# Two output products as seven block products with sums built in DRAM, and state-space tiles four slots apart

## The chip, the cores and the metric

One core of a Trainium2 chip runs one layer of a decoder trunk in float32. The metric is device microseconds of one execution; the median of three runs stands for a kernel. TensorE multiplies, VectorE and ScalarE (ACT) do elementwise work, GpSimd (POOL) does a little, SyncE (SP) issues the DMA transfers. The engines work through their instructions in order, each on its own, and wait for each other by semaphores.

## The reference, cut to what matters

Sequence T = 512, model width D = 1024, hidden width 2816.

```python
z = rms_norm(x, norm_mix) @ w_in                # u | conv | q k v | three gates
merged = (g[..., 0:D] * (y_ssm @ w_branch[0]) + g[..., D:2*D] * (y_conv @ w_branch[1])
          + g[..., 2*D:] * (y_attn @ w_branch[2]))
x = x + merged @ w_out
hf = rms_norm(x, norm_ffn) @ w_ffn_in
x = x + (silu(hf[..., :FFN]) * hf[..., FFN:]) @ w_ffn_out
x = x + sigmoid(rms_norm(x, norm_ple) @ w_ple_gate) * (p @ w_ple_proj)
return rms_norm(x, norm_final)
```

`y_ssm` is a complex-diagonal state-space model over time with a gated output, `y_conv` a short convolution, `y_attn` a sliding-window attention.

## The kernel before, in words

**Products.** Every float32 operand of TensorE is split in a high part (`hi`, a cast to float32r on ACT) and a low part (`lo`, the subtraction on VectorE), and a product is three matmuls: high x high, high x low, low x high (`mm3`, L247; `td_mm`, L1213).

**Weight stream.** `add_slab` lists slabs of at most 1 MB in the order of use; `emit_load` (L179) issues their DMA on SP into one of two `raw` buffers; `emit_split` (L187) casts one half (128 x 1024) on ACT (L206) and sets its subtraction on VectorE (L207) four pumps later. A pump is one k step of a tile, three matmuls. Four buffers hold split halves during the first part; from w_out on, three more. A half is split as soon as a buffer is free: `take`, `group`, `ahead` and `retire` count it. So SP runs ahead of the work by two raw buffers and the split halves.

**Order of the work.** It is written out by hand. `later(d, fn)` puts a piece of work d pumps later into an engine's queue, `peq` holds small TensorE pieces that a pump puts between the matmuls of a stage, and `slot()` marks the steps of the branch stages: one slot after each gate tile or branch pair, 27 before the GLU, each eight pumps.

**State-space tiles.** Four tiles of 128 channels (`ssm_gen`, L957) run beside the branch stages, begun at slots 0, 5, 10 and 15 (L1127) and taken one step further by every slot. A step each: loads of `tb` and `uu`; the table E; the table W with the load of `cs` and the transposes; the matmuls into `vps` with the rotation and the scan behind them (`vsw`, `G`, `R`, `gsw`, `sv`); two steps later the copy of `Dg` on ACT (L1075); then the output matmuls `y_one` (L1082, L1084), after which SP stores `sy` (L1092), loads `un` and, waiting for the stores, loads `yr` (L1098); four steps after that `yc` and its GELU. After the slots the gated output (GLU) of the state-space branch, the last gates and its branch product follow.

**w_out and w_ffn_out.** `td_gemm` (L1230) computes [token, d] products: for each half n of the 1024 columns, four token tiles of 128, kn steps of k, three matmuls of 512 columns a step. For n = 0 the four tiles share each weight half, for n = 1 a tile is finished before the next one (where a norm follows) so that the tile's RMS norm (`Norm.pre`, L1253) begins at once: square on ACT (L1261), mean on VectorE (L1264), power -0.5 on POOL (L1265), scale on VectorE (L1272), transposes on TensorE (L325), high and low parts. `accum` (L1209) adds a finished tile into `xr` (L1211). w_out has kn = 8; the SwiGLU has hidden tiles in chunks of 8, 8 and 6, each chunk a run of w_ffn_in tiles (`g` halves, silu, product) and a `td_gemm` with w_ffn_out. `xr` is loaded from x when the buffers of the branch stage are free (L1205).

Of the kernel before, what the change touches and what calls it, by code (L numbers as in the profile page):

```python
# [25 lines left out]
WARM = 3  # L26
PREP_RATE = 1.7
# [48 lines left out]
def hybrid_trunk_kernel(  # L76
# [44 lines left out]
    def add_slab(ap, k, n, axis):  # L121
        s = len(slabs)
        slabs.append(dict(ap=ap, k=k, n=n, raw=None))
        cnt = 2 if k * n == 2048 else 1
        for i in range(cnt):
            halves.append(dict(s=s, i=i, cnt=cnt, axis=axis, hl=None))
# [31 lines left out]
    for n in range(2):  # L158
        for kk in range(2):
            add_slab(kn(w_out[0][kk * 512:kk * 512 + 512, n * 512:n * 512 + 512]), 4, 512, "k")  # L160
    CHUNKS = [(0, 8), (8, 8), (16, 6)]
    for h0, hn in CHUNKS:
        for j in range(h0, h0 + hn, 2):
            for ab in range(2):
                c0 = ab * FFN + j * 128
                add_slab(kn(w_ffn_in[0][:, c0:c0 + 256]), 8, 256, "n")
        for n in range(2):
            for k0 in range(0, hn, 4):
                kq = min(4, hn - k0)
                r0 = (h0 + k0) * 128  # L170
                add_slab(kn(w_ffn_out[0][r0:r0 + kq * 128, n * 512:n * 512 + 512]), kq, 512, "k")
# [5 lines left out]
    state = dict(pump=0, delay=False, split=0, load=0, next=0, top=3, slot=0, pools=[hla] * 4)  # L177

    def emit_load():  # L179
        s = slabs[state["load"]]  # L180
        state["load"] += 1
        t = rawp.tile([128, 2048], F32, tag="raw", name="raw")
        v = t[:, 0:s["k"] * s["n"]].rearrange("p (k n) -> p k n", k=s["k"])
        sp.dma_start(out=v, in_=s["ap"])
        s["raw"] = v

    def emit_split():  # L187
# [5 lines left out]
        k, n, i = s["k"], s["n"], h["i"]  # L193
        if h["cnt"] == 1:
            src = s["raw"]
        elif h["axis"] == "n":
            n //= 2
            src = s["raw"][:, :, i * n:(i + 1) * n]
        else:
            k //= 2  # L200
            src = s["raw"][:, i * k:(i + 1) * k, :]
        pl = state["pools"][state["slot"] % len(state["pools"])]
        state["slot"] += 1
        hi = pl.tile([128, 1024], F32R, tag="hi", name="hi").rearrange("p (k n) -> p k n", k=k)
        lo = pl.tile([128, 1024], F32R, tag="lo", name="lo").rearrange("p (k n) -> p k n", k=k)
# [60 lines left out]
    def pump(tick=True):  # L266
        if tick:
            state["pump"] += 1
            run_due(state["pump"])
# [117 lines left out]
    def prep_gen(tp):  # L387
        # per-channel vectors: ssm_d (4 tiles) and the conv taps (3 x 4 tiles)
# [59 lines left out]
    def prep_fine(tp, lt, ldt, T1, T2, tabs):  # L448
# [73 lines left out]
        # coefficients  # L522
# [85 lines left out]
    # the tensor engine's clock rises only under load  # L608
# [347 lines left out]
    # chunks of 4 tokens; channels of a group pair and the time in the chunk share the partitions  # L956
    def ssm_gen(ct):  # L957
# [69 lines left out]
        # the two row halves of the array write to banks of their own  # L1027
# [52 lines left out]
        def y_one(a):  # L1080
# [16 lines left out]
            yr = sp_.tile(SC, F32, tag="yb", name="yr", bufs=1)  # L1097
            sp.dma_start(out=yr, in_=sy_d[rows, :].rearrange("p (i c) -> p i c", i=4))  # L1098
            svs["un"], svs["yr"] = un, yr
# [3 lines left out]
        yield  # L1103
        yield
        yield
        yield
        un, yr = svs["un"], svs["yr"]
# [19 lines left out]
    SSM_SLOTS = {0: 0, 5: 1, 10: 2, 15: 3}  # L1127
# [17 lines left out]
    def branch(d0, sgs, yh, yl, mode, mh=None, ml=None):  # L1145
        hl = take()
        for i in range(2):
# [8 lines left out]
            if mode == 2:  # L1156
                split_ap(merged[:, d], mh[:, d], ml[:, d])
# [11 lines left out]
    drain()  # L1169
    ysh, ysl = ybox[0]  # L1170
# [16 lines left out]
    mst = ExitStack()  # L1187
    mhp = open_pool(mst, "mhl", side="right")
    mh = mhp.tile([128, KD, T], F32R, tag="mh", name="mh")
    ml = mhp.tile([128, KD, T], F32R, tag="ml", name="ml")  # L1190
    sg1 = gates()
    branch(0, sg0, yfh, yfl, 2, mh, ml)
    branch(2, sg1, yfh, yfl, 2, mh, ml)
    for d0 in (4, 6):
        branch(d0, gates(), yfh, yfl, 2, mh, ml)
# [4 lines left out]
    xp = open_pool(ctx, "xres")  # L1200
    hlb = open_pool(ctx, "hlb", 3)
    state["pools"] = [hla] * 4 + [hlb] * 3
    state["slot"] = 4
# [14 lines left out]
    def td_outer_k(ah, al, kn_, n):  # L1218
        pss = [ps_z() for _ in range(4)]
        for h in range(kn_ // 2):  # L1220
            hi, lo = take()
            for t in range(4):
                for k in range(2):
                    kk = 2 * h + k
                    td_mm(pss[t], ah, al, kk, slice(t * 128, (t + 1) * 128), hi, lo, k, kk == kn_ - 1)
                    pump()
        for t in range(4):
            accum(t, n, pss[t])

    def td_gemm(ah, al, kn_, pre_fn=None):  # L1230
        td_outer_k(ah, al, kn_, 0)
# [190 lines left out]
```

## Time and profile before

| | us |
|---|---|
| runs | 894.74, 895.66, 896.30 (median 895.66) |
| span of the profiled execution, first to last instruction | 892.6 |
| the execution's own time beside its span | not given apart; the median is 3.06 above the span |
| TensorE busy | 874.4 (98% of the span) |
| VectorE, ACT, POOL busy | 491.1, 341.0, 95.9 |
| w_out stage | about 424 to 470 |
| SwiGLU stage | about 471 to 838 |

How to read it: a matmul's duration in the profile is pipelined, its interval to the next one is its price. Idle time stands in brackets behind an instruction with what ended it. A wait for several things is put down to the last. Where an instruction's engine has other work in its queue, the instruction waits its turn though all that it needs is there.

### The profile page before, as it was taken

Reading aid. Unit: us, or ns where it says so; the run is one execution under the profiler, and the core shown is the slowest. Engines: PE = TensorE matmul, PEld = TensorE weight load, DVE = VectorE, ACT = ScalarE, POOL = GpSimd, SP = SyncE. Lnnn points to the kernel's source line nnn. Section 1 sums busy time; section 2 is a strip of 40 time slices with the busy share of each in tenths; the row PEclk is TensorE's granted clock in tenths of the full one; section 3 lists DMA queues with packets and bytes.
Section 4 is the critical chain, followed back from the end, with each engine's and each line's share of the span. In section 5 each row is a group of like instructions: output and inputs, shape, how many; then the busy total and the mean of one; then the engine's idle time right before and its main releaser. Section 6 shows DMA issues by size and latency. Waiting matters only on the chain.

```text
span 892.6 us, 10527 instructions
## 1 busy us (share of the span) xinstructions
PE 874.4 (98%) x4143; PEld 715.2 (80%) x4143; DVE 491.1 (55%) x737; ACT 341.0 (38%) x546; POOL 95.9 (11%) x86
## 2 busy tenths in 40 slices
PE   8999999999999979999999999999999999999997
PEld 6988787877777758888889888888888888888886
DVE  3789698948588585554545433333333333334654
ACT  5665556445443343433334322212222212222533
POOL 1030061713123030000000000000000000000000
PEclk9999999999999989999999999999999999999998
DMA  8756511253634523223813322222225332233002
GB/s 300 216 189 218 195 59 30 66 173 113 178 95 156 156 94 107 95 79 134 284 46 107 130 94 95 95 95 94 95 95 211 99 100 87 72 120 110 29 1 94
DMA packets 84849, 107.25 MB, mean 120 GB/s; under 512 B 6120, under 2 KB 66176, under 8 KB 84288
## 3 DMA queue, kind: packets, MB, share of 16 engines
q1 hardware_dynamic: 84800, 106.59, 36.5%
q8 instruction: 32, 0.52, 0.2%
q14 instruction: 17, 0.14, 0.1%
HBM read 94.83 MB, written 11.55 MB: 119 GB/s over the span
## 4 chain that ended last, share of the span: by engine, by line
PE 77%; DVE 10%; issue 4%; ACT 3%; DMA 3%; SPq 1%; POOL 1%; POOLq 0%; DVEq 0%; ACTq 0%
PE z L248 17%; PE z L249 16%; PE z L250 16%; PE z L1216 8%; PE z L1215 8%; PE z L1214 8%; DVE lo L207 1%; DVE s_t L839 1%; DMA xt<-in_x_dram 1%; PE t L325 1%; DVE s_t L812 1%; DMA raw<-in_w_in_dram 1%; POOL gsw L1063 1%; ACT s_t L826 1%; PE t L1084 1%
## 5 line engine op out<-in xcount | busy, mean ns | idle before, releaser
L248 PE MATMUL z<-h,hi 128*128 128x512 f32 (+1 forms) x776 | 298.6, 385 | 0.0
L207 DVE TENSOR_TENSOR lo<-raw,hi 128x1024 fp32r<-128x1024 f32 x142 | 177.6, 1253 | 216.2 <-ACT hi L206 216.1
L249 PE MATMUL z<-l,hi 128*128 128x512 f32 (+1 forms) x776 | 292.2, 377 | 0.0
L250 PE MATMUL z<-h,lo 128*128 128x512 f32 (+1 forms) x776 | 292.1, 376 | 0.0
L206 ACT CAST hi<-raw 128x1024 fp32r<-128x1024 f32 x142 | 148.2, 1047 | 133.1 <-PE z L1216 87.2
L248 PEld LDWEIGHTS z<-h,hi 128*128 128x128 f32 x776 | 146.8, 189 | 29.9 <-issue 3.7
L250 PEld LDWEIGHTS z<-h,lo 128*128 128x128 f32 x776 | 146.7, 189 | 27.6
L249 PEld LDWEIGHTS z<-l,hi 128*128 128x128 f32 x776 | 147.0, 189 | 24.7
L1214 PE MATMUL z<-hi,gh 128*128 128x512 f32 x176 | 69.5, 395 | 0.0
L1216 PE MATMUL z<-hi,gl 128*128 128x512 f32 x176 | 69.1, 393 | 0.0
L1215 PE MATMUL z<-lo,gh 128*128 128x512 f32 x176 | 69.1, 392 | 0.0
L1265 POOL TENSOR_TENSOR rs<-ms,nhalf 128x1 f32<-128x1 f32 x8 | 4.4, 550 | 487.2 <-DVE ms L1264 487.2
L244 ACT CAST gh<-sil 128x512 fp32r<-128x512 f32 x22 | 13.6, 620 | 86.0 <-DVE sil L1319 86.0
L248 PE MATMUL z<-yh,hi 128*128 128x512 f32 x112 | 45.1, 403 | 0.0
L249 PE MATMUL z<-yl,hi 128*128 128x512 f32 x112 | 44.2, 395 | 0.1
L250 PE MATMUL z<-yh,lo 128*128 128x512 f32 x112 | 44.2, 395 | 0.0
L1310 ACT ACTIVATE sil<-z 128x512 f32<-128x512 f32 x22 | 13.2, 598 | 75.4 <-PE z L250 75.4
L1319 DVE TENSOR_TENSOR sil<-z,sil 128x512 f32<-128x512 f32 x22 | 15.2, 691 | 46.8 <-PE z L250 46.8
L1216 PEld LDWEIGHTS z<-hi,gl 128*128 128x128 f32 x176 | 33.1, 188 | 7.5
L1215 PEld LDWEIGHTS z<-lo,gh 128*128 128x128 f32 x176 | 33.1, 188 | 7.4
L1214 PEld LDWEIGHTS z<-hi,gh 128*128 128x128 f32 x176 | 33.1, 188 | 7.3
L1211 DVE TENSOR_TENSOR xr<-z,xr 128x512 f32<-128x512 f32 x32 | 21.5, 687 | 15.6 <-PE z L1216 15.5
(258 smaller groups left out, 1058.5 us busy)
## 6 DMA issues: line engine op xcount, KB each, us to landing
raw<-in_w_in_dram SPq DMA_DIRECT2D x23, 1024.0 KB, 5.5
raw<-in_w_ffn_in_dram SPq DMA_DIRECT2D x22, 1024.0 KB, 5.2
raw<-in_w_ffn_out_dram SPq DMA_DIRECT2D x10, 1024.0 KB, 5.0
raw<-in_w_branch_dram SPq DMA_DIRECT2D x12, 512.0 KB, 3.4
cs<-tb SPq DMA_DIRECT2D x4, 1024.0 KB, 5.2
raw<-in_w_out_dram SPq DMA_DIRECT2D x4, 1024.0 KB, 5.8
raw<-in_w_ple_gate_dram SPq DMA_DIRECT2D x4, 1024.0 KB, 5.1
xt<-in_x_dram SPq DMA_DIRECT2D x4, 512.0 KB, 9.4
```

What stands on the lines that cost most here:

```text
L206: act.copy(out=hi, in_=src)
L207: todo = [lambda: dve.tensor_tensor(lo, src, hi.bitcast(F32), ALU.subtract)]
L244: act.copy(out=hi, in_=src)
L248: pe.matmul(ps, wh, ah, start=first, stop=False)
L249: pe.matmul(ps, wh, al, start=False, stop=False)
L250: pe.matmul(ps, wl, ah, start=False, stop=last)
L1211: dve.tensor_tensor(dst, ps, dst, ALU.add)
L1214: pe.matmul(ps, ah[:, kk, ts], hi[:, k, ns], start=(kk == 0), stop=False)
L1215: pe.matmul(ps, ah[:, kk, ts], lo[:, k, ns], start=False, stop=False)
L1216: pe.matmul(ps, al[:, kk, ts], hi[:, k, ns], start=False, stop=last)
L1310: act.activation(out=s, in_=ps, func=AF.Silu)
L1319: dve.tensor_tensor(sil[i], ps, sil[i], ALU.mult)
```

## The change

Write a product A B with A cut in four blocks by token half and by even or odd 128-row tile of k, and B in four by the same k and by column half n. Seven products of blocks, with sums of blocks on either side, give all four blocks of the result (Winograd's form); the seven results go with signs into two to four accumulators in PSUM and from there into `xr`.

- Left side: `forms` splits, for each pair of 128-row tiles, seven blocks of 128 x 256 in place of two of 128 x 512, three of them the blocks themselves and four sums on VectorE. It stands where `split_ap` stood for `merged` and for the SwiGLU product.
- Right side: four sums of weight blocks, t1 to t4, are built in DRAM by transfers on POOL's queue, eight for each of the four products (w_out and three chunks): two copies, two adding transfers on them, a copy of t1 into t2, an adding one, a copy of t2 into t4, an adding one. After the state-space tiles are drained, one is issued every 12 pumps; before the first slab of a product is loaded, all eight of it are issued.
- `block_product` takes the place of `td_gemm`: seven products of two token tiles and kt = 4, 4, 4, 3 steps, each with a slab of its own (two halves; 2 and 1 steps for kt = 3). Where a norm follows, the norms of token tiles 0 and 1 are begun after the fifth product and those of 2 and 3 after the seventh, four pumps apart.
- Four buffers of split halves stay until w_ple_gate, where three more are opened. The gain of the last norm and `ppt` are loaded after the last block product, not within the second chunk.
- State-space tiles begin at slots 0, 4, 8 and 12; `yr` is loaded a step after `un`, and `yc` comes three steps after the output matmuls in place of four.

```diff
+SUM_EVERY = 12
+NORM_GAP = 4
...
+    A11, A12, A22, FD, S2, S3, S4 = range(7)
+    ORDER = (A11, FD, S2, S4, S3, A12, A22)
+    ORDER_NORM = (A11, FD, S2, S4, A12, S3, A22)
+    def add_block_product(w, r0, kt, order):
...
+        op(t1, blk(0, 1))
+        op(t3, blk(0, 1))
+        op(t1, blk(0, 0), True)
+        op(t3, blk(1, 1), True)
+        op(t2, t1)
+        op(t2, blk(1, 1), True)
+        op(t4, t2)
+        op(t4, blk(1, 0), True)
+        sums.append(ops)
+        right = {A11: blk(0, 0), A12: blk(1, 0), A22: t4, FD: t1, S2: t2, S3: t3, S4: blk(1, 1)}
+        for f in order:
+            add_slab(right[f], kt, 512, "k", 8 * len(sums))
...
     def emit_load():
+        while n_sum - len(sum_ops) < s["need"]:
+            sum_ops.popleft()()
...
     def pump(tick=True):
+            if state["sums"] and sum_ops and state["pump"] % SUM_EVERY == 0:
+                sum_ops.popleft()()
...
         for a in range(4):
             peq.append(lambda a=a: y_one(a))
         yield
+        yr = sp_.tile(SC, F32, tag="yb", name="yr", bufs=1)
+        sp.dma_start(out=yr, in_=sy_d[rows, :].rearrange("p (i c) -> p i c", i=4))
         yield
         yield
-        yield
...
-    SSM_SLOTS = {0: 0, 5: 1, 10: 2, 15: 3}
+    SSM_SLOTS = {0: 0, 4: 1, 8: 2, 12: 3}
...
+    def forms(g, i):
+        sums = fmp.tile([128, 4, 256], F32, tag="sums", name="sums")
+        g11, g12, g21, g22 = (g[:, h, o:o + 256] for o in (0, 256) for h in range(2))
+        split_ap(g[:, :, 0:256], fh[:, 0:2, i], fl[:, 0:2, i])
+        dve.tensor_tensor(sums[:, 0], g21, g22, ALU.subtract)
+        dve.tensor_tensor(sums[:, 1], sums[:, 0], g11, ALU.subtract)
+        dve.tensor_tensor(sums[:, 2], g11, g21, ALU.subtract)
+        dve.tensor_tensor(sums[:, 3], g12, sums[:, 1], ALU.add)
+        split_ap(sums, fh[:, 3:7, i], fl[:, 3:7, i])
+        split_ap(g22, fh[:, 2, i], fl[:, 2, i])
...
+    PRODUCTS = {A11: (0, True, ((1, 0, 0),)), FD: (1, True, ((1, 1, 1),)), S2: (0, False, ((-1, 0, 1),)),
+                S4: (1, False, ((1, 0, 1),)), S3: (0, False, ((-1, 1, 1),)), A12: (2, True, ((1, 0, 0),)),
+                A22: (0, False, ((1, 1, 0),))}
+    PRODUCTS_NORM = {**PRODUCTS, S3: (0, False, ((-1, 1, 1), (1, 1, 0))), A22: (3, True, ((1, 1, 0),))}
+    def block_product(kt, norm=None):
...
+                for t in range(2):
...
+                        pe.matmul(ps, fh[:, f, kk, ts], hi[:, k], start=st, stop=False, skip_group_check=True)
+                        pe.matmul(ps, fh[:, f, kk, ts], lo[:, k], start=False, stop=False, skip_group_check=True)
+                        pe.matmul(ps, fl[:, f, kk, ts], hi[:, k], start=False, stop=last, skip_group_check=True)
+                        pump()
+                    if last:
+                        for sign, th, n in goes:
+                            dst = xr[:, 2 * th + t, n * 512:(n + 1) * 512]
+                            dve.tensor_tensor(dst, ps if sign > 0 else dst, dst if sign > 0 else ps,
+                                              ALU.add if sign > 0 else ALU.subtract)
+                retire(h0)
+            if norm is not None and i in (4, 6):
+                for t in range(2):
+                    norm.pre(2 * (i // 5) + t, NORM_GAP * t)
...
-    td_gemm(mh, ml, 8, nf.pre)
+    block_product(4, nf)
...
-            td_gemm(gh, gl, hn, npl.pre)
+        block_product(hn // 2, npl if ci == 2 else None)
```

## Rows read from the trace of the kernel before

**Rows 1.** The page's table: busy us (share of the span), instructions of each engine.

```profile
PE 874.4 (98%) x4143; PEld 715.2 (80%) x4143; DVE 491.1 (55%) x737; ACT 341.0 (38%) x546; POOL 95.9 (11%) x86
```

**Rows 2.** L1214 in two stages (ns min/median/max, first, last start); timeline with transposes.

```profile
L1214 PE MATMUL z<-hi,mh x64: 388/393/477, 424.0 to 469.5; 128*128 128x512 f32 x64
...
L1214 PE MATMUL z<-hi,gh x64: 389/392/398, 560.8 to 604.3; 128*128 128x512 f32 x64
...
457.77 0.39 PE L1216 MATMUL z<-hi,ml 128*128 128x512 f32 x1
458.00 0.60 PE L325 MATMUL t<-cst,xn 128*128 128x128 f32 x4
458.36 0.47 PE L1214 MATMUL z<-hi,mh 128*128 128x512 f32 x1
```

**Rows 3.** Waits of TensorE: us in total, times, longest.

```profile
PE t L1082 <- ACT Dg L1075: 4.5, 1, 4.5
```

**Rows 4.** Timeline of TensorE: an undisturbed tile, and around that wait.

```profile
219.89 0.50 PE L248 MATMUL z<-h,hi 128*128 128x512 f32 x1
...
221.37 0.50 PE L248 MATMUL z<-h,hi 128*128 128x512 f32 x1
...
319.26 0.39 PE L248 MATMUL z<-h,hi 128*128 128x512 f32 x1
...
324.61 0.80 PE L1082 MATMUL t<-uu,Dg 128*128 128x128 f32 x2 [4.49 <-ACT Dg L1075]
...
333.72 0.39 PE L248 MATMUL z<-h,hi 128*128 128x512 f32 x1
```

**Rows 5.** Windows: PE, PEld, DVE, ACT, POOL busy us (x), PEclk, DMA share, GB/s.

```profile
290.00:300.00 10.00, 10.00 (x52) 8.08 (x52) 9.54 (x12) 5.64 (x11) 1.44 (x1) 1.00 0.12 25
...
320.00:330.00 10.00, 5.23 (x17) 3.32 (x17) 7.63 (x10) 5.27 (x9) 4.13 (x3) 0.68 0.33 105
```

**Rows 6.** Timeline of SP's issues and of ACT before the wait.

```profile
295.16 4.91 SPq L1092 DMA_DIRECT2D sy<-ys  x8
...
301.42 0.34 SPq L1098 DMA_DIRECT2D yr<-sy  x1
...
302.28 0.43 SPq L184 DMA_DIRECT2D raw<-in_w_in_dram  x1
...
310.03 1.05 ACT L206 CAST hi<-raw 128x1024 fp32r<-128x1024 f32 x1 [12.39 <-DMA raw<-in_w_in_dram]
```

**Rows 7.** Groups by form: out<-in, count | busy us, mean ns | idle before.

```profile
L207 DVE TENSOR_TENSOR lo<-raw,hi 128x1024 fp32r<-128x1024 f32 x142 | 177.6, 1253 | 216.2 <-ACT hi L206 216.1
L206 ACT CAST hi<-raw 128x1024 fp32r<-128x1024 f32 x142 | 148.2, 1047 | 133.1 <-PE z L1216 87.2 <-DMA raw<-in_w_in_dram 19.8 <-PE z L249 16.3
...
L1211 DVE TENSOR_TENSOR xr<-z,xr 128x512 f32<-128x512 f32 x32 | 21.5, 687 | 15.6 <-PE z L1216 15.5
...
L245 DVE TENSOR_TENSOR l<-t,h 128x512 fp32r<-128x512 f32 x24 | 15.9, 684 | 2.4 <-ACT h L244 2.4
...
L1272 DVE SCALAR_TENSOR_TENSOR xn<-xr,rs,g 128x1024 f32<-128x1024 f32 x8 | 10.3, 1285 | 3.8 <-POOL rs L1265 3.6
...
L1265 POOL TENSOR_TENSOR rs<-ms,nhalf 128x1 f32<-128x1 f32 x8 | 4.4, 550 | 487.2 <-DVE ms L1264 487.2
```

**Rows 8.** xr: issue (SP's timeline), landing (the page), VectorE's adds (line L1211).

```profile
424.14 0.37 SPq L1205 DMA_DIRECT2D xr<-in_x_dram  x1
...
xr<-in_x_dram SPq DMA_DIRECT2D x1, 2048.0 KB, 7.9
...
L1211 DVE TENSOR_TENSOR xr<-z,xr x32: 678/691/693, 443.2 to 840.3; 128x512 f32<-128x512 f32 x32
```

**Rows 9.** All slab loads (tile raw): us from issue to landing.

```profile
DMA to landing us min/median/max: 3.2/5.2/11.6
```

**Rows 10.** Windows with xr's load and of the first w_ffn_out chunk (columns as rows 5).

```profile
427.50:430.00 2.50, 2.50 (x12) 2.01 (x11) 1.88 (x2) 2.48 (x3) 0.00 (x0) 1.00 1.03 418
...
560.50:605.00 44.50, 44.50 (x195) 36.30 (x194) 15.66 (x17) 8.92 (x9) 0.00 (x0) 1.00 0.33 106
```

More of the change, by code (lines that the diff above doesn't have):

```diff
@@ L119, in hybrid_trunk_kernel, with add_slab @@
     slabs = []
-    def add_slab(ap, k, n, axis):
+    def add_slab(ap, k, n, axis, need=0):
         s = len(slabs)
[L123 to L126, printed above, removed]
+        slabs.append(dict(ap=ap, k=k, n=n, raw=None, need=need))
+        if k * n <= 1024:
+            parts = [(0, k, 0, n)]
+        elif axis == "n":
+            parts = [(0, k, i * (n // 2), n // 2) for i in range(2)]
+        else:
+            k1 = (k + 1) // 2
+            parts = [(0, k1, 0, n), (k1, k - k1, 0, n)]
+        for q in parts:
+            halves.append(dict(s=s, part=q, hl=None))
     def kn(ap):
@@ L166, in hybrid_trunk_kernel @@
                 add_slab(kn(w_ffn_in[0][:, c0:c0 + 256]), 8, 256, "n")
[L167 to L171, printed above, removed]
+        add_block_product(w_ffn_out[0], h0 * 128, hn // 2, ORDER_NORM if hn == 6 else ORDER)
     for n in range(2):
@@ L176, in hybrid_trunk_kernel @@
     due = {}
-    state = dict(pump=0, delay=False, split=0, load=0, next=0, top=3, slot=0, pools=[hla] * 4)
+    state = dict(pump=0, delay=False, split=0, load=0, next=0, top=3, slot=0, pools=[hla] * 4, sums=False)
+    sum_ops = deque()
+    for ops in sums:
+        sum_ops.extend(ops)
+    n_sum = len(sum_ops)
     def emit_load():
@@ L1169, in hybrid_trunk_kernel @@
     drain()
+    state["sums"] = True
     ysh, ysl = ybox[0]
@@ new lines, in hybrid_trunk_kernel @@
+    PRODUCTS_NORM = {**PRODUCTS, S3: (0, False, ((-1, 1, 1), (1, 1, 0))), A22: (3, True, ((1, 1, 0),))}
+    def block_product(kt, norm=None):
+        banks = {}
+        for i, f in enumerate(ORDER if norm is None else ORDER_NORM):
+            bk, first, goes = (PRODUCTS if norm is None else PRODUCTS_NORM)[f]
+            if first:
+                banks[bk] = [(ps_t if bk == 2 else ps_z)() for _ in range(2)]
+            for q in range(2):
+                h0 = group(1)
+                if q == 0:
+                    ahead()
+                hi, lo = halves[h0]["hl"]
+                k0, kc = halves[h0]["part"][0:2]
+                for t in range(2):
+                    ps, ts = banks[bk][t], slice(t * 128, (t + 1) * 128)
+                    for k in range(kc):
+                        kk = k0 + k
+                        st = first and kk == 0
+                        last = kk == kt - 1
+                        pe.matmul(ps, fh[:, f, kk, ts], hi[:, k], start=st, stop=False, skip_group_check=True)
[11 more added lines that the diff above has]
+                    norm.pre(2 * (i // 5) + t, NORM_GAP * t)
@@ L1318, in hybrid_trunk_kernel @@
                     ps = z_tile()
[L1319 to L1327 removed]
+                dve.tensor_tensor(g[:, i], ps, g[:, i], ALU.mult)
+            forms(g, j // 2)
+        block_product(hn // 2, npl if ci == 2 else None)
     fst.close()
+    fmst.close()
+    hlb = open_pool(ctx, "hlb", 3)
+    state["pools"] = [hla] * 4 + [hlb] * 3
+    state["slot"] = 4
     ep = open_pool(ctx, "ple")
+    gain = load_gain(norm_final, ep)
+    ppt = ep.tile([128, 4, D], F32, tag="ppt", name="ppt")
+    for t in range(4):
+        sp.dma_start(out=ppt[:, t], in_=pp_d[t * 128:(t + 1) * 128, :])
     xg = ep.tile([128, 4, D], F32, tag="xg", name="xg")
```

110 lines of the change are left out of this document (30 added, 80 removed).

## The prediction

> **What bounds the kernel now.** I read the busy table first: TensorE is busy 874.4 of the 892.6 us of the span, every other engine under 56% [rows 1]. Only two things can then gain: fewer matmuls, or an end to a stretch in which TensorE stands still. The second view is one matmul line over one stage. In w_out 192 matmuls run, and the 64 of the first kind start between 424.0 and 469.5 us; 189 intervals less four groups of norm transposes (four matmuls each; they stretch an interval from 0.23 to 0.59 us, so 0.36 a group) give (45.5 - 1.4) / 189 = 0.233 us each. In the first w_ffn_out chunk 43.5 / 189 = 0.230 us [rows 2]. The 0.39 us shown as duration of one is pipelined and is no price. The third view is TensorE's waits: one is large, 4.5 us before the output matmuls of a state-space tile (L1082), waiting for the ACT copy of Dg [rows 3]. The timeline shows what it cost: from 319.26 to 333.72 us TensorE did one triple and four pairs of tile unit and triple. Such a pair takes 221.37 - 219.89 = 1.48 us where nothing waits, so the work is worth 0.69 + 4 x 1.48 = 6.6 us and took 14.5: **7.9 us lost** [rows 4]. The slice around it has a granted clock of 0.68: after the idle 4.5 us part of it ran at 1.2 instead of 2.4 GHz, which is the other 3.4 us [rows 5].
>
> Why it waited: SP stood in order behind the stores of the tile before (sy, issued from 295.16), then waited for their landing before yr, then issued cs, a 1 MB load, and only at 302.28 the next weight slab. ACT, in order too, waited 12.39 us for that slab and copied vsw, gsw and Dg of the last tile late [rows 6].
>
> **The change, part by part.**
>
> *Matmuls.* Seven products of 2 token tiles x kt x 3 replace eight. w_out: 168 for 192. w_ffn_out: 7 x 2 x 11 x 3 = 462 for 528. 24 x 0.233 + 66 x 0.230 = 5.6 + 15.2 = **-20.8 us**, all of it on the path.
>
> *State-space tiles every four slots, yr one step later, yc one earlier.* Tile 3 now begins at slot 12, not 15. Its cs load is issued in the step in which the former tile's output matmuls are only queued, so ahead of the sy stores; the wait for sy comes a slot later, behind weight loads. This takes out both things that stood ahead of the late slab. Bounds: 0 (the wait moves to another tile) to 7.9 us. I take **-7.9**, since the row names one chain and both its causes move. Speaking against: VectorE is 95% busy in a slice of this stage [rows 5], and the same work now falls into four slots in place of five.
>
> *More weight splits.* Every product has a slab of its own: 28 slabs in 56 halves, for 16 slabs in 30 halves. A half is one ACT cast (1.05 us) and one VectorE subtraction (1.25 us) [rows 7]. TensorE takes 12 x 0.23 = 2.8 us for a half, so both fit. Adds into xr rise from 32 to 60, at 0.69 us. Per product of kt = 4 VectorE has 2 x 1.25 + 2 x 0.69 = 3.9 us under 5.6 us of TensorE: cost nothing while the slabs come in time; without that cover each late half is a TensorE wait.
>
> *Forms of the left side.* A pair of 128-row tiles is split in 1,792 columns, not 1,024, with four sums of 128x256: at most 2.8 us more for the sums, 1 us for the splits, under some 17 to 22 us of TensorE. Only the last pair shows: A11 comes to that pair's low part 17 matmuls, 3.9 us, after its start (14, 3.2 us, for kt = 3), while multiply, four sums and the low part are 0.69 + 4 x 0.35 + 0.69 = 2.8 us of VectorE (the sums an estimate, half of a 128x512 row) plus what stands in its queue, at most one weight subtraction. 0 to 1.2 us at each of four starts; I take 0.5 each: **+2**.
>
> *xr.* It is issued when the last branch matmul is done (424.14 us) and lands 7.9 us later [rows 8]. Before, its first use was at 443.2 us [rows 8]. Now A11 is added 5.6 us into w_out, so VectorE stands still until about 432 us, and behind its two adds (1.4) and one subtraction (1.25) stands the third slab's first low half, which TensorE wants at 423.9 + 11.2 = 435.1. 432 + 2.7 = 434.7: just in time, 0 to 3 us late if the sums share the DMA engines. I take **+1**.
>
> *The norms.* Before, token tiles finish one by one with no weight subtraction near. Now tiles 0 and 1 finish together after the fifth product. VectorE's queue from there to the low part of tile 1 that the first w_ffn_in matmuls read: one add 0.7, four adds of S3 2.75, three weight subtractions 3.7, two scales 2.6, two small ones 0.3, three low parts of h 2.05, one add of A22 0.7, and 1.9 of gaps at its beginning: 14.7 us [rows 7]. TensorE arrives after two products and four transpose groups, 11.1 + 1.4 = 12.5 us. So **+2** there. At w_ple_gate the products are 4.2 us: VectorE needs by the same count 12 us to tile 0's low part, TensorE is there after 9.5: **+3** with the halves behind it. Bounds for the two together: 0 (queues kinder than my order) to 2 x 7.9, a wait of 4.5 us with the clock lost, as in [rows 4]. POOL's power for each norm (0.55 us) [rows 7] stands in w_out behind the sums in POOL's queue, which adds 0 to 3.3 us there (next part); I take 0.
>
> *The sums in DRAM.* 32 transfers of 1 MB (0.75 MB for the last eight), half of them adding, on POOL's queue; each reads what an earlier one wrote, so POOL waits in front of it. No row shows such a transfer. From the nearest rows: a copy is 5.2 us at the median of the slab loads, 11.6 at the worst [rows 9]; an adding one reads twice, so 5.2 to 15.6 (three passes of 5.2). One is issued every 12 pumps of three matmuls, 8.3 us; so POOL is held 0 to 3.3 us by a copy. The first slab of w_out is loaded five halves (40 of 96 pumps) ahead, at pump 56; four sums are out by then and four are issued at once. The first adding one goes out at pump 36, 25 us. With 11.6 and 15.6, t2 is whole 68 us and t4 95 us after the sums' start; w_out starts at 67 us, wants t2 as third product at 78 and t4 as seventh at 100, each less some 5 to 7 us of loading and splitting. So even the dear end hardly costs; I take 0. Later blocks have 128 pumps more. The Trainium skill's DMA: Bandwidth & Descriptors, § Anatomy of one DMA, fits a transfer from POOL as 2.0 us plus bytes at 436 GB/s; by it a copy would be an estimated 4.4 us, and no run here shows it.
>
> *Moved loads.* norm_final's gain and ppt now wait for the last product and stand on SP ahead of one w_ple_gate slab. 2.5 MB need some 10 us by xr's row [rows 8]; ppt's first tile is wanted after 6, and the slab only for the second half, after 22: VectorE may wait, TensorE not. 0, at most 1. Four weight buffers in place of seven: the gate stages run on four already.
>
> **Sum.** -20.8 - 7.9 + 2 + 1 + 2 + 3 = -20.7. Against the profiled span 892.6 gives 871.9; what lies around the span is 895.66 - 892.6 = 3.1 us against the median of the runs, so 875.0. A difference within 0.2% (1.8 us) can't be told from none.
>
> **Rivals.**
> 1. *The tile's stall moves* (VectorE too dense in four slots): 875 + 7.9 = 883. For: the 95%. Against: y_one keeps its four slots after the rotation is queued. 0.18.
> 2. *VectorE becomes the bound at the norms*, two idle stretches with the lower clock behind them: 875 - 5 + 15.8 = 886. For: 14.7 over 12.5. 0.12.
> 3. *Weight slabs come late beside the sums.* While xr loads, the DMA engines are at 1.03 of their time and 418 GB/s, against 0.33 in a w_ffn_out chunk [rows 10]. If slabs land at 11.6 us [rows 9] in w_out and chunk 0, two buffers give one slab in (11.6 + 4.5) / 2 = 8 us against 5.6; three slabs per stage lack a lead: 2 x 3 x 2.4 = 15, so 890. The Trainium skill's DMA: Bandwidth & Descriptors, § Issuing engines are not separate DMA queues, says that transfers from POOL and SP run on the same 16 engines and interleave; it speaks for this rival, and no row here has two queues of data at once. 0.11.
> 4. *Slower: the chain of sums starves w_out.* t1, t2, t4 follow one another with three adding steps; with 11.6 for a copy and a for an add, t4 is whole at 48 + 3a us, wanted at 95 (100 less the load). From about a = 23 us the wait eats the gain of 20.7; at 30 us it is 138 - 95 = 43: 918. Against: 1 MB in 30 us is 35 GB/s, and the slab loads do 200. 0.11, and 0.03 for other losses of this size.
> 5. *It doesn't do what it says:* saved matmuls, the same time, because something slower feeds them. VectorE's 3.9 of 5.6 us per product speaks against it: 895. 0.04.
>
> **Numbers.** The forecast has 0.41: 875, with its own range 868 to 881. Faster: 0.41 + 0.18 + 0.12 + 0.09 of rival 3 = 0.80. Same: 0.04 + 0.02 of rival 3 = 0.06. Slower 0.14. The range: below, all of 20.8 + 7.9 with hardly a cost, 867; above, rival 3 whole, 890. That leaves out rivals 4 and 5, 0.18.
>
> **What would show it.** 630 matmuls in the products; no wait over 1 us at L1082; first adds into xr waiting for xr's DMA near 430; TensorE idle about 2 to 3 us before the first w_ffn_in and w_ple_gate matmuls, waiting for low parts of h; POOL's transfers of 5 to 16 us; slabs in w_out still landing under 8 us. Wrong it is if TensorE waits on weight halves inside a product, or SP waits for POOL's transfers.

## The result, and the profile after

| | before | after |
|---|---|---|
| median of four runs, us | 895.20 (893.41 to 896.30) | 878.29 (876.95 to 879.97) |
| ratio | | 0.982, 95% interval 0.9803 to 0.9837 |
| span of the profiled execution, us | 892.6 | 875.6 |

Faster by 16.9 us; the forecast was 20.7, and the time lies 3.3 us above the number and inside the range. The difference of the spans, 17.0 us, can be laid out by stage. A stage is taken from the first start of one matmul line to the first start of the next one:

| stage | before | after | difference | of it fewer matmuls |
|---|---|---|---|---|
| start to w_out | 424.0 | 419.3 | -4.7 | |
| w_out and first w_ffn_in run | 136.8 | 132.9 | -3.9 | -5.6 |
| chunk 0 (w_ffn_out and next w_ffn_in run) | 132.4 | 126.2 | -6.2 | -5.5 |
| chunk 1 | 110.3 | 104.5 | -5.8 | -5.5 |
| chunk 2 (w_ffn_out) | 35.1 | 30.5 | -4.6 | -4.1 |
| w_ple_gate, first to last matmul | 47.0 | 55.0 | +8.0 | |
| end | 7.0 | 7.2 | +0.2 | |

The table of the page, which answers to [rows 1], and its line on POOL's transfers:

```profile
PE 853.4 (97%) x4053; PEld 697.1 (80%) x4053; DVE 561.4 (64%) x866; ACT 376.6 (43%) x587; POOL 125.9 (14%) x118
...
T<-in_w_ffn_out_dram POOLq DMA_DIRECT2D x12, 1024.0 KB, 11.5
raw<-T SPq DMA_DIRECT2D x12, 1024.0 KB, 6.7
...
T<-in_w_out_dram POOLq DMA_DIRECT2D x6, 1024.0 KB, 9.9
```

TensorE has 90 instructions fewer and 21.0 us less busy time; VectorE has 129 more, ACT 41 more. The sums, copies and adding ones together, take a median of 9.9 and 11.5 us from issue to landing, a slab of sums 6.7 us to be loaded.

TensorE's matmuls of the products, by line (each line is one of the three of `mm3`; count, duration, first and last start), to be held against [rows 2]:

```profile
L1289 PE MATMUL z<-hi,fh x180: 391/394/482, 419.3 to 812.7; 128*128 128x512 f32 x180
L1289 PE MATMUL t<-hi,fh x30: 393/394/398, 441.7 to 803.4; 128*128 128x512 f32 x30
```

(180 + 30) x 3 = 630, as the change says.

TensorE's waits (total us, times, longest), to be held against [rows 3]:

```profile
PE t L1071 <- ACT ET L1031: 2.2, 2, 1.1
PE t L362 <- DVE l L280: 1.5, 2, 1.2
...
PE z L1263 <- DVE l L280: 1.2, 1, 1.2
PE z L1262 <- DVE lo L242: 1.2, 1, 1.2
...
PE t L1121 <- DVE sv L1102: 1.0, 2, 0.5
```

The wait of 4.5 us for Dg is gone. In its place stand small ones in the tiles: 2.2 us for ET, the transposed table E, and 1.0 us for `sv`. At w_ple_gate stand new ones, small in this list; the timeline of TensorE there shows where they lie:

```profile
813.43 0.39 PE L1261 MATMUL z<-hi,h 128*128 128x512 f32 x1
...
815.02 0.49 PE L1262 MATMUL z<-lo,h 128*128 128x512 f32 x1 [1.20 <-DVE lo L242]
...
816.75 0.50 PE L1263 MATMUL z<-hi,l 128*128 128x512 f32 x1 [1.24 <-DVE l L280]
...
826.02 0.63 PE L362 MATMUL t<-cst,xn 128*128 128x128 f32 x4 [0.83 <-DVE xn L1326]
...
832.41 0.66 PE L362 MATMUL t<-cst,xn 128*128 128x128 f32 x4 [1.25 <-DVE l L280]
```

These waits come to 4.5 us; the stage lost 8.0. The windows (us of the stretch, busy time of PE, PEld, DVE, ACT, POOL, then granted clock, DMA share, GB/s) have a slice at a lower clock right after the first two:

```profile
815.00:820.00 5.00, 3.74 (x15) 2.86 (x16) 5.00 (x7) 0.01 (x1) 0.00 (x0) 0.76 0.55 168
820.00:825.00 5.00, 5.00 (x21) 3.95 (x19) 1.92 (x4) 3.90 (x6) 0.55 (x1) 0.89 0.99 382
```

From this row one would blame the clock. A second profile of the same kernel (below) has no matmul in this stage above 505 ns, where this one has 776, and the granted clock is 1.00 in both slices:

```profile
815.00:820.00 5.00, 3.79 (x21) 3.21 (x22) 5.00 (x7) 0.00 (x0) 0.00 (x0) 1.00 0.62 219
820.00:825.00 5.00, 3.40 (x14) 2.13 (x12) 1.91 (x4) 4.41 (x8) 0.55 (x1) 1.00 1.02 379
```

Its stage is as long all the same, 54.7 us, with one wait more (1.1 us for a low part of h, at 824.0), and the transposes of token tile 2 come at 825.5, as they come at 826.0 here: what is not lost to the clock is waited for instead. In the first slice of both profiles VectorE is full and ACT does nothing. Behind ACT's idle time stands this, in the timeline of ACT:

```profile
811.12 1.03 ACT L241 CAST hi<-raw 128x1024 fp32r<-128x1024 f32 x1
...
813.01 2.00 ACT L241 CAST hi<-raw 128x1024 fp32r<-128x1024 f32 x2
821.10 1.05 ACT L241 CAST hi<-raw 128x1024 fp32r<-128x1024 f32 x1 [6.09 <-DMA raw<-in_w_ple_gate_dram]
...
822.53 1.06 ACT L1315 ACTIVATE xn<-xr 128x1024 f32<-128x1024 f32 x1
```

ACT waits 6.09 us for the third w_ple_gate slab, and the square of token tile 2, which needs nothing but `xr` (its last add ends near 817.3 us on VectorE), stands behind that cast in its queue.

The third thing to see is POOL's timeline from the end of the state-space tiles on:

```profile
329.10 1.67 POOL L184 DMA_DIRECT2D T<-in_w_out_dram  x2
335.39 1.21 POOL L184 DMA_DIRECT2D T<-in_w_out_dram  x1 [4.63 <-DMA T<-in_w_out_dram]
...
396.18 0.52 POOL L184 DMA_DIRECT2D T<-T  x1 [6.51 <-DMA T<-in_w_ffn_out_dram]
405.17 1.16 POOL L184 DMA_DIRECT2D T<-in_w_ffn_out_dram  x1 [8.48 <-DMA T<-T]
449.90 1.47 POOL L1319 TENSOR_TENSOR rs<-ms,nhalf 128x1 f32<-128x1 f32 x1 [43.57 <-DVE ms L1318]
```

The code issues a sum every 12 pumps, but that sets only their place in POOL's queue. POOL waits for nothing else there, so 14 sums go out in the 76 us from 329.1 to 405.2, each as soon as the one it reads has landed, and then POOL stands 43.57 us before the first norm's power.

### The profile page after: what moved, and what is told of

Same layout as the page of the kernel before. It is cut to its first block, busy times and chain, and to the rows that moved or that the text cites. A ratio compares the mean times of both kernels' runs of the same rounds, so it can differ in the third digit from the quotient of the medians.

```text
span 875.6 us, 10663 instructions
## 1 busy us (share of the span) xinstructions
PE 853.4 (97%) x4053; PEld 697.1 (80%) x4053; DVE 561.4 (64%) x866; ACT 376.6 (43%) x587; POOL 125.9 (14%) x118
## 3 DMA queue, kind: packets, MB, share of 16 engines
q0 software_dynamic: 10240, 31.46, 15.1%
## 4 chain that ended last, share of the span: by engine, by line
PE 72%; DVE 13%; issue 5%; ACT 5%; DMA 3%; POOL 2%; SPq 0%; POOLq 0%; DVEq 0%; ACTq 0%
PE z L283 17%; PE z L284 17%; PE z L285 17%; PE z L1290 3%; PE z L1289 3%; PE z L1291 3%; DVE lo L242 2%; PE z L1263 1%; PE z L1262 1%; PE z L1261 1%; PE z L679 1%; DVE s_t L876 1%; DVE s_t L849 1%; ACT hi L241 1%; PE t L1071 1%
## 5 line engine op out<-in xcount | busy, mean ns | idle before, releaser
L242 DVE TENSOR_TENSOR lo<-raw,hi 128x1024 fp32r<-128x1024 f32 (+1 forms) x168 | 204.0, 1218 | 136.6 <-ACT hi L241 136.1
L241 ACT CAST hi<-raw 128x1024 fp32r<-128x1024 f32 (+1 forms) x168 | 171.1, 1030 | 150.9 <-PE z L284 26.7
L1289 PE MATMUL z<-hi,fh 128*128 128x512 f32 x180 | 71.7, 398 | 0.0
L1290 PE MATMUL z<-lo,fh 128*128 128x512 f32 x180 | 71.3, 396 | 0.0
L1291 PE MATMUL z<-hi,fl 128*128 128x512 f32 x180 | 71.2, 395 | 0.0
L1365 DVE TENSOR_TENSOR g<-z,g 128x512 f32<-128x512 f32 x22 | 15.2, 692 | 57.0 <-PE z L285 57.0
L284 PE MATMUL z<-yl,hi 128*128 128x512 f32 x112 | 44.2, 395 | 0.1
L285 PE MATMUL z<-yh,lo 128*128 128x512 f32 x112 | 44.2, 395 | 0.0
L1291 PEld LDWEIGHTS z<-hi,fl 128*128 128x128 f32 x180 | 33.8, 188 | 8.4 <-DVE fl L280 0.2
L1290 PEld LDWEIGHTS z<-lo,fh 128*128 128x128 f32 x180 | 33.8, 188 | 8.2 <-DVE lo L242 0.4
L1289 PEld LDWEIGHTS z<-hi,fh 128*128 128x128 f32 x180 | 33.8, 188 | 7.8
L1357 ACT ACTIVATE g<-z 128x512 f32<-128x512 f32 x22 | 13.2, 599 | 51.5 <-PE z L285 51.5
## 6 DMA issues: line engine op xcount, KB each, us to landing
T<-in_w_ffn_out_dram POOLq DMA_DIRECT2D x12, 1024.0 KB, 11.5
```

Source lines behind the costliest of these rows:

```text
L241: act.copy(out=hi, in_=src)
L242: todo = [lambda: dve.tensor_tensor(lo, src, hi.bitcast(F32), ALU.subtract)]
L284: pe.matmul(ps, wh, al, start=False, stop=False)
L285: pe.matmul(ps, wl, ah, start=False, stop=last)
L1289: pe.matmul(ps, fh[:, f, kk, ts], hi[:, k], start=st, stop=False, skip_group_check=True)
L1290: pe.matmul(ps, fh[:, f, kk, ts], lo[:, k], start=False, stop=False, skip_group_check=True)
```

## The experiments

Times are compared with runs of the kernel before on the same chip. Line numbers in a view are those of the kernel that it shows, so one statement can have several.

**One part alone: the tiles.** The kernel before with only this edit (and `yr` and `yc` moved as in the change):

```diff
-    SSM_SLOTS = {0: 0, 5: 1, 10: 2, 15: 3}
+    SSM_SLOTS = {0: 0, 4: 1, 8: 2, 12: 3}
```

> The kernel before with the state-space edits alone (slots 0, 4, 8, 12; yr a step later, yc a step earlier). Theory A, from the two traces: the 7.9 us lost at L1082 go, and 3.1 us of new small waits (copy of ET, sv) come, so about 4.7 us less, 890.5, a ratio of 0.9948. Theory B, the forecast's own term: 7.9 us less, 887.3, ratio 0.991, and the 3.1 us belong to the products. Theory C: what the w_out start gained in the changed kernel has another source; then nothing, ratio 1.000.

890.96 against 895.39: 0.9948 [0.9927, 0.9968], so 4.7 us. TensorE's waits in this kernel:

```profile
PE t L1034 <- ACT ET L994: 2.2, 2, 1.2
...
PE t L1084 <- DVE sv L1065: 1.0, 2, 0.5
```

The same two as in the changed kernel: they belong to the denser tiles, and not to the products. The part brings 4.7 us (2.9 to 6.5 by the interval) and not 7.9.

**The other part alone: the products.** The changed kernel with the tiles as before (slots 0, 5, 10, 15, and `yr`, `yc` as they were).

> The changed kernel with the state-space edits undone. Theory A: the two parts add up, so the 4.5 us wait and its low clock are back and the products alone give 17.0 - 4.7 = 12.3 us: 882.9, ratio 0.9863. Theory B (an interaction: the tiles' earlier end is what lets the sums begin in time): less than 8 us of gain, ratio over 0.991, with waits for weight slabs in w_out.

890.51: 0.9945 [0.9925, 0.9965], only 4.9 us. By these ratios the two parts bring 4.7 and 4.9 us alone; together they bring 16.1 by the ratio above and 14.9 in a second measurement (below); by its interval each of these is good to some 2 us. The old wait at L1119 is back with 4.7 us, as it should be, but another has come, inside w_out (waits, then the timelines of POOL, SP and TensorE):

```profile
PE t L1119 <- ACT Dg L1112: 4.7, 1, 4.7
PE z L1290 <- ACT hi L241: 2.8, 1, 2.8
```

```profile
350.83 1.67 POOL L184 DMA_DIRECT2D T<-in_w_out_dram  x2
...
429.10 1.16 POOL L184 DMA_DIRECT2D T<-in_w_ffn_out_dram  x1 [10.43 <-DMA T<-T]
```

```profile
423.63 0.38 SPq L1253 DMA_DIRECT2D xr<-in_x_dram  x1
```

```profile
444.13 0.49 PE L1290 MATMUL z<-hi,fh 128*128 128x512 f32 x1 [2.78 <-ACT hi L241]
```

With the tiles ending later, the sums begin at 350.8 in place of 329.1 and the fourteenth is issued at 429.1, 5.5 us after the load of `xr`, not at 405.2. Sums, `xr` and two w_out slabs then share the DMA engines, and a weight half comes late. That is rival 3 of the prediction, in a kernel that lacks the other half of the change.

**The same without the sums.** As the last one, with no sum transfers and each slab loaded from a plain block of the weights.

```diff
-        sums.append(ops)
-        right = {A11: blk(0, 0), A12: blk(1, 0), A22: t4, FD: t1, S2: t2, S3: t3, S4: blk(1, 1)}
+        sums.append([])
+        right = {A11: blk(0, 0), A12: blk(1, 0), A22: blk(1, 0), FD: blk(0, 1), S2: blk(1, 1), S3: blk(1, 1), S4: blk(1, 1)}
```

> The products alone (state-space tiles as before), with no sums issued; the slabs of t1 to t4 are read from plain weight blocks, so that part of the computation is left out. The trace of the products alone has a wait of 2.8 us for a slab in w_out, while POOL issues a sum at 429 us beside xr's load; in the changed kernel POOL had issued its sums by 405 us. Theory A: POOL runs its sums as fast as they land, so the tiles' earlier end moves them out of the way of xr and the w_out slabs; without sums the products alone give their full 12 us: about 883, ratio 0.986, no wait for slabs in w_out. Theory B: the wait comes from xr and two raw buffers alone: ratio stays near 0.9945.

882.47 against 894.68: 0.9864 [0.9844, 0.9885], against 0.9945 with the sums. No wait inside w_out is left; the wait for Dg still has its 4.7 us. So the sums cost about 0.0081 x 895 = 7.3 us where they lie beside `xr`; in the traces w_out, to the first w_ffn_in matmul, takes 48.0 us with them and 41.5 without. This kernel also reads its slabs from other places, but the changed kernel reads the summed slabs and has 41.5 us too. In the changed kernel the earlier end of the tiles takes them out of that place: this is why the parts together bring 5 to 6.5 us more than their sum.

**The changed kernel again,** beside the kernel without sums and those with held sums and with fewer adds (below).

> The changed kernel itself once more, as the yardstick of this chip: ratio 0.980 to 0.984 if chips agree.

879.62, 0.9834 [0.9814, 0.9853], span 875.0; w_ple_gate 54.7 us.

**Longer products ahead of the last norms.** The chunk of 6 first, so that the last products have four steps of k, 5.6 us in place of 4.2, over which VectorE may do its queue:

```diff
-    CHUNKS = [(0, 8), (8, 8), (16, 6)]
+    CHUNKS = [(0, 6), (6, 8), (14, 8)]
```

> The changed kernel with the hidden chunks in the order 6, 8, 8, so that the last block product has kt = 4 and 5.6 us a product in place of 4.2. Theory A: what TensorE loses at w_ple_gate (about 7.3 us) is VectorE's queue of adds, subtractions and norm between the fifth product and the low part of h; with 2.8 us more of TensorE under the same work the first wait (2.7 us) and the lower clock behind it (1.7) go: 4 to 6 us less than the changed kernel, about 873, ratio 0.976. Theory B: the waits come from the loads moved there (gain, ppt on SP) or from late w_ple_gate slabs: no change, 878, ratio 0.982.

887.95, 0.9923 [0.99, 0.9946]: slower than the changed kernel. The stage of w_ple_gate did get shorter, 51.4 for 55.0, but a new wait came in chunk 0 (waits; timelines of TensorE, ACT and SP):

```profile
PE z L1289 <- ACT hi L241: 5.6, 1, 5.6
```

```profile
551.86 0.80 PE L1289 MATMUL z<-hi,fh 128*128 128x512 f32 x1 [5.56 <-ACT hi L241]
```

```profile
550.77 1.56 ACT L241 CAST hi<-raw 128x1024 fp32r<-128x1024 f32 x2 [11.36 <-DMA raw<-in_w_ffn_out_dram]
```

```profile
539.34 0.38 SPq L226 DMA_DIRECT2D raw<-in_w_ffn_out_dram  x1
```

A slab issued at 539.34 is cast at 550.77; it took 11.3 us to land, where such slabs (0.75 MB) take 4.7 us at the median in the changed kernel. Two sums were issued at 534.6 and 536.9 and landed at 543.6 and 552.3, beside it and the slab after it. The short chunk at the front starts earlier and meets the last sums. In the changed kernel sums run beside chunk 0 too (issued at 545.6, 554.2 and 559.0), but one at a time, and a slab of 9.7 us there makes no wait. The Trainium skill's DMA: Bandwidth & Descriptors, § Issuing engines are not separate DMA queues, says that transfers of POOL and SP run on the same 16 engines and interleave; this slab beside two sums agrees, with 11.3 us for 4.7.

**The same with the last eight sums held back** until chunk 0's product is done, by a small POOL instruction that reads `xr` ahead of them:

```diff
-            if state["sums"] and sum_ops and state["pump"] % SUM_EVERY == 0:
+            if state["sums"] and len(sum_ops) > state["hold"] and state["pump"] % SUM_EVERY == 0:
...
+        if ci == 0:
+            gate = sm.tile([128, 1], F32, tag="gate", name="gate")
+            pool.tensor_tensor(gate, xr[:, 3, 512:513], nhalf, ALU.mult)
+            state["hold"] = 0
```

> Chunks in the order 6, 8, 8, with the last eight sums held behind the first chunk's block product by a small POOL instruction that reads xr. Theory A (sums beside a block product make its slabs land late: 11.4 us, 5.6 us of wait and the lower clock behind it): the wait goes, and with the shorter wait at w_ple_gate it is 3 to 4 us under the changed kernel: ratio 0.977 to 0.979. Theory B (two raw buffers can't feed products of kt = 3 in any case): it stays near 0.992.

874.58 against 894.68: 0.9777 [0.9761, 0.9792], against 0.9834 of the changed kernel beside it. The wait in chunk 0 is gone; w_ple_gate takes 50.7 us. With the sums out of its way the slab is in time: it was they that made it late, and not the other chunk order by itself. What is left is `PE t L362 <- DVE xn L1326` with 3.7 us, of which 2.1 lie at w_ple_gate and 1.6 at the norm behind w_out.

**Less work in VectorE's queue at the last norms.** The prediction had put the loss at w_ple_gate down to VectorE: 12 us of queue against 9.5 us of TensorE. Here the four adds of S3 in the last chunk are left out, 2.75 us of that queue:

```diff
-                    if last:
+                    if last and not (norm is not None and kt == 3 and f == S3):
```

> The changed kernel with the four adds of product S3 in the last chunk left out (2.75 us of VectorE between the fifth product and w_ple_gate), a part of the computation. Theory A (VectorE's queue makes the waits at w_ple_gate): the first waits and the lower clock behind them go, 3 to 5 us less than the changed kernel, ratio about 0.978. Theory B (gain, ppt and w_ple_gate loads make them): no change against the changed kernel.

878.14, 0.9817 [0.9796, 0.9837]; the changed kernel beside it had 0.9834. The stage stays at 54.8 us, and the waits stay with it. VectorE now idles for the norm itself, and its mean is formed at 811.50, where the changed kernel has it at 811.67 with four adds more ahead of it (timeline of VectorE, then of ACT):

```profile
811.50 0.15 DVE L1318 TENSOR_SCALAR ms<-ss 128x1 f32<-128x1 f32 x1 [1.90 <-ACT xn L1315]
```

```profile
809.37 1.05 ACT L241 CAST hi<-raw 128x1024 fp32r<-128x1024 f32 x1 [2.29 <-DMA raw<-in_w_ple_gate_dram]
810.33 1.05 ACT L1315 ACTIVATE xn<-xr 128x1024 f32<-128x1024 f32 x1
...
821.10 1.05 ACT L241 CAST hi<-raw 128x1024 fp32r<-128x1024 f32 x1 [5.82 <-DMA raw<-in_w_ple_gate_dram]
```

The square of token tile 1 comes right behind a cast that waited for the first w_ple_gate slab, and the cast of the third slab waits at 821.10 as before. So VectorE's queue is not what alone was late: in the changed kernel that square and the adds end some 0.5 us apart, and shortening one of two that are equally late brings next to nothing. What a shorter queue brings once ACT is out of the way, this run doesn't show.

**The cast behind the squares.** The new theory was ACT's order. The split ahead in the first two tiles of the w_ple_gate stage is left to the third, so that no cast that waits for a slab stands ahead of the squares of tiles 2 and 3:

```diff
         for t in range(4):
-            ahead()
+            if n or t > 1:
+                ahead()
```

> The changed kernel; in the w_ple_gate stage the casts of the third slab are put behind the first two token tiles. In the trace ACT stands 5.8 us in front of that slab (its load stands behind gain and ppt on SP), and the squares of token tiles 2 and 3 stand behind it. Theory A: that in-order wait on ACT makes the later waits of TensorE at w_ple_gate (about 3 us of transposes waiting for xn and l): 2 to 4 us less than the changed kernel, ratio about 0.980 where that one has 0.9834. Theory B: VectorE's queue makes them: no change, 0.983.

874.07 against 894.56: 0.9769 [0.9755, 0.9783], some 4 to 6 us better than the changed kernel by the medians. The profiled execution shows 2.3 to 2.6 of it, the shorter stage; what the others gained beyond that isn't shown. The two later waits of TensorE, 0.83 and 1.25 us for `xn` and its low part, are gone; the two near the first matmul, for low parts from VectorE, are still there with 2.4 us and a lower clock behind them (0.86 and 0.80 granted in the slices from 815 to 825). The stage takes 52.4 us. The third slab's load stands ahead of gain and `ppt` on SP (issued at 816.1, 816.6 and 817.1 in the changed kernel), not behind them as was expected. In ACT's timeline the squares now follow the casts that are ready:

```profile
814.08 2.00 ACT L241 CAST hi<-raw 128x1024 fp32r<-128x1024 f32 x2
818.87 1.06 ACT L1315 ACTIVATE xn<-xr 128x1024 f32<-128x1024 f32 x1
...
820.65 1.06 ACT L1315 ACTIVATE xn<-xr 128x1024 f32<-128x1024 f32 x1
```

**Both of these.** The last edit with the other chunk order and the held sums.

> The version with chunks 6, 8, 8 and the last sums held, with the casts of the third w_ple_gate slab put behind the first two token tiles as well. Theory A: the 3.7 us that transposes wait for xn there go: 871 to 872, ratio 0.974. Theory B: 874.6, ratio 0.978.

870.88 against 894.56: 0.9734 [0.972, 0.9748], span 870.4, the fastest of all. The stage and the medians agree here: 3.7 us each off the kernel with held sums, though only 2.1 us of the wait that the expectation named stood at this place. From 800 us to the end TensorE waits 0.33 us once, and w_ple_gate takes 47.0 us, the length it had in the kernel before:

```profile
L1261 PE MATMUL z<-hi,h x72: 221/389/481, 816.3 to 863.3; 128*128 128x512 f32 x56, 128*128 128x384 f32 x8, 128*128 128x128 f32 x8
```

**The waits for ET.** In the changed kernel with the transposes of E put first in `peq` in place of last:

```diff
-        peq.append(e_tr)
+        peq.appendleft(e_tr)
```

> The changed kernel with the transposes of a tile's table E put ahead of the output matmuls of the tile before in TensorE's queue of small pieces. Theory A: the 2.2 us that TensorE waits for the copy of ET come from both tiles' pieces falling in one slot; then 1.5 to 2.5 us less than the changed kernel, 876, ratio 0.979. Theory B: VectorE is simply too dense in four slots, the waits move elsewhere: 878, ratio 0.982.

891.15, 0.9946 [0.9925, 0.9967], much slower than the changed kernel. The waits for ET are gone, but E itself is not there yet, and TensorE, in order, waits for it:

```profile
PE t L1030 <- DVE E L1019: 12.3, 3, 5.2
```

From w_out on it takes 456.0 us, as the changed kernel does (456.3); all of the loss is in the tiles. So with E first in `peq` TensorE waits longer, for what ET is made from; a place in between was not tried.

**Only the move of yr and yc.** The kernel before with tiles still five slots apart:

```diff
-            yr = sp_.tile(SC, F32, tag="yb", name="yr", bufs=1)
-            sp.dma_start(out=yr, in_=sy_d[rows, :].rearrange("p (i c) -> p i c", i=4))
...
         yield
+        yr = sp_.tile(SC, F32, tag="yb", name="yr", bufs=1)
+        sp.dma_start(out=yr, in_=sy_d[rows, :].rearrange("p (i c) -> p i c", i=4))
         yield
         yield
-        yield
```

> The kernel before with yr a step later and yc a step earlier, tiles still five slots apart. Theory A: what held the slab back was the wait for sy in front of cs on SP; then the 4.5 us wait at L1082 and its low clock go without the spacing: 887 to 889, ratio 0.991 to 0.993. Theory B: it is SP's wait for ys in front of all of them, which only the spacing moves: the wait stays, ratio 1.000.

910.26 against 894.56: 1.018 [1.0166, 1.0194], **slower** by 15.7 us, which neither theory had. The wait for Dg comes three times and is nearly four times as long in all (waits; timeline of ACT):

```profile
PE t L1082 <- ACT Dg L1075: 16.5, 3, 6.3
```

```profile
250.59 0.63 ACT L1120 ACTIVATE qq<-qq 128x512 f32<-128x512 f32 x1 [2.11 <-DVE qq L1117]
254.17 0.62 ACT L244 CAST yh<-yu 128x512 fp32r<-128x512 f32 x1 [2.94 <-DVE yu L1121]
...
255.18 0.82 ACT L1075 COPY Dg<-dbuf 64x256 f32<-64x256 f32 x2
```

Before, `yc` of tile i comes at slot 5i + 10, step 5 of the next tile. One step earlier it is at 5i + 9, step 4 of the next tile, and its sigmoid and cast, which wait for VectorE, stand ahead of that tile's copy of Dg on ACT. With tiles four apart the same move gives 4i + 9, which is step 5 again.

**The same coincidence in the fast kernel.** The fastest kernel with `yc` one step earlier still, 4i + 8, so step 4 of the next tile:

```diff
         yield
-        yield
         un = svs["un"]
```

> The version before this one, with yc and its GELU one slot earlier (two steps after the output matmuls), so that they fall between the steps of the two other tiles. Theory A: the copy of ET on ACT waits behind the cast of yu, which waits for VectorE; apart, the 2.1 us of waits for ET go: 1.5 to 2.5 us less than that version, ratio 0.972. Theory B: yr comes too late for it and SP and VectorE wait for it: no gain or a loss, ratio 0.974 to 0.978.

889.28, 0.9931 [0.9919, 0.9944]: 17.6 us lost, by the ratios, on the kernel it is made from. The waits have the same row as the experiment before:

```profile
PE t L1119 <- ACT Dg L1112: 16.5, 3, 6.4
```

Two kernels that share only this step of `yc` show 16.5 us in three waits each, and the kernels with it on step 5 show at most one wait there. So `yc` can't come one step earlier without the closer tiles. The later `yr` with `yc` left in its place, and the closer tiles without that move, were not tried.

## Why the prediction was right or wrong

**Fewer matmuls: right.** Taken to the first matmul of what follows, the three products of w_ffn_out became shorter by 44.2 - 39.2 = 5.0, 44.2 - 39.2 = 5.0 and 35.1 - 30.5 = 4.6 us, 14.6 in all, 0.7 of them transposes that now lie behind w_ple_gate's first matmul. Against 66 x 0.230 = 15.2 this is the step that carried the sum: the interval of the matmuls as the price, not their 0.39 us.

**Costs at the starts of the products (+2) and of xr (+1): mostly the right size, at another place.** TensorE waits at none of the starts in chunks 0 and 1, but the matmuls of these products come every 0.233 us and not every 0.230, so that 15.2 + 0.7 - 14.6 = 1.3 us are lost in the three, where 1.5 had been set against them. `xr` (+1) cost TensorE nothing. What the prediction did not have is that the w_ffn_in runs behind chunks 0 and 1, with as many matmuls as before, became shorter too: 87.1 for 88.3 us and 65.3 for 66.1, so 2.0 us. Both come with the products and without the closer tiles as well; why, no run shows. In w_out and the w_ffn_in run behind it the costs come to 5.6 - 3.9 = 1.7 us, where the start, `xr` and the norms had 3.5 together.

**State-space tiles (-7.9): the mechanism right, the size off.** The wait for Dg went, and with it the low clock behind it. But the branch stage gained 4.7 us, and 4.7 with this part alone. The step that failed is "I take -7.9, since the row names one chain and both its causes move": it took the upper bound as if nothing came after the stall. Four slots for the work of five leave TensorE waiting for ET and `sv` (2.2 + 1.0 us in one list), so about 3.2 of the 7.9 us came back as small waits. That this gives 4.7 to the tenth is luck: kernels with the same tiles reach w_out between 418.9 and 422.5 us in their traces. What I had put down against it, VectorE at 95% of a slice, fits these waits; that it is their cause was argued and not tested. That a rival gave the whole 7.9 to a stall that moves was too dear as well.

**The norm at w_ple_gate (+3): the mechanism there, a dearer one missed.** It cost 8.0 us, 0.7 of them two more groups of transposes. The step "VectorE needs by the same count 12 us to tile 0's low part, TensorE is there after 9.5" came out nearly so: counted from the sixth product's first matmul at 804.1, VectorE has that low part ready at 816.7, after 12.6 us, and TensorE is there at 813.4, after 9.3. These are the two waits of 2.4 us near the first matmul, and longer products take them away. But the step has the wrong bound for the stage. ACT stands 6.09 us in front of the third slab with the squares of two token tiles behind that cast, and up to their transposes this hides the rest, the lower clock too. Taking the cast from ahead of the squares gave 4 to 6 us by the medians (2.3 to 2.6 in the trace), and 3.7 with longer products; what then remains, the waits for VectorE and the clock behind them, went with the longer products. I had counted the work of each engine at that place, but not what stands in ACT's order ahead of it and waits. The prediction's "Moved loads" did ask about the w_ple_gate slabs, but only whether TensorE would want them late, and found 22 us of room. It missed that ACT, which has to cast them, is in order and has the norm's squares behind them. On SP the third slab is issued at 816.1, when the low half of the first one has been taken (813.75 to 816.1 on VectorE) and its buffer is free, so VectorE's queue has a part in this wait as well.

**How near the sum came is in part luck.** By the spans it was 17.0 us and not 20.7. The tiles fell short by 3.2 us and the last norm by 5.0; against them stand 2.0 us of shorter w_ffn_in runs that nobody had forecast, 1.8 at w_out and the first norm, and 0.9 in the three chunks' products, 0.7 of which only moved to the last norm.

**Rival 3, 0.11: did not come, but is real.** Slabs in the changed kernel come in time, though one of w_ffn_in takes 18.1 us beside sums: inside the products TensorE has no large wait. Without the earlier tiles it has one, of 2.8 us, and with the short chunk first one of 5.6. The price of an adding sum was bounded well, 5.2 to 15.6 us from [rows 9] and 9.0 to 15.1 measured for 1 MB; a copy of a weight block was not, 5.2 to 11.6 set and 6.0 to 14.8 measured. What failed is the step "One is issued every 12 pumps of three matmuls, 8.3 us": POOL ran them one behind the other, 14 in 76 us, one in 5.4. It did no harm, and the early start is what kept them from `xr`. The prediction priced the two parts as independent, and they aren't: 4.7 + 4.9 alone, 15 to 16 together. By the fit that the prediction cited from the Trainium skill's DMA: Bandwidth & Descriptors, § Anatomy of one DMA, a copy of 1 MB would take an estimated 4.4 us; the copies from one sum to another took 7.1 us here at the median, beside other loads, so the measurement decides.

**Rivals 1, 2, 4 and 5.** No stall of the old size is in the tiles (rival 1); TensorE lost 8.0 us at one norm, not two stretches of 7.9 us for VectorE (rival 2). The chain of sums never kept w_out waiting in the changed kernel (rival 4), and the saved matmuls came through whole (rival 5).

**Not settled.** Why ET and `sv` are still waited for was not taken apart further than that E comes late from VectorE. A third `raw` buffer, which would let the third w_ple_gate slab be loaded earlier, was not tried, nor was the late split in the chunk order of before with held sums, nor a cast of the first w_ple_gate slab put behind the square of token tile 1.

## What to carry to other kernels

Before a norm or any small step on a latency path, look in the queue of each engine that it uses for an instruction that waits for a transfer: the busy time of the engine says nothing about it. Here moving one such cast on an engine 43% busy gave 4 to 6 us, and taking 2.75 us of work off the engine that was full gave nothing clear of the noise while the other stood. POOL, with nothing else to wait for, ran the transfers at the pace of their landings, whatever pace the code lists them in; say by a real dependence where they may not run. When a change has several parts, run each alone: here two that look independent were worth 9.6 us apart and 15 to 16 together, and half of an edit that gained 4.7 us cost 15.7 by itself.

## What the runs showed of the hardware that I had not expected

An instruction of an in-order engine that lands one step earlier can cost far more than its length: 0.6 us of ACT's sigmoid and 0.6 us of its cast, ahead of a copy that TensorE waits for, made the whole kernel 15.7 us slower in one run and 17.6 in another. And transfers within DRAM were slower than loads of the same size on SP, whether they add or not: of 1 MB each, those that add a weight block took 10.8 us at the median (9.0 to 15.1), plain copies of a weight block, issued in pairs, 11.9 (6.0 to 14.8), and copies of one sum to another 7.1, against 5.1 to 5.6 for the loads. So it is not shown that the adding is what costs. Beside them loads were late in turn: 11.3 us for a slab of 4.7, and up to 18.1 in w_ffn_in, where TensorE did not wait for it.
